# A 64 B store per partition between two large loads of a streaming multiply-and-GELU kernel

## Chip, cores, metric

One core of one Trainium2 chip. The time is device microseconds of one execution; most executions agree within 0.3%. A ratio is the mean time of one kernel's runs over that of the other's of the same rounds, so it is not quite the ratio of the medians quoted beside it.

## The reference

```python
def reference(x, y):                 # both 1024 x 4096 float32
    z = x * y
    return (0.5 * z * (1 + np.tanh(np.sqrt(2 / np.pi) * (z + 0.044715 * z ** 3)))).astype(np.float32)
```

Two arrays of 16.8 MB are read and one is written. There are few operations for each byte.

## The kernel before

Each of 128 partitions holds 8 rows, 32768 floats. The whole of x lies in SBUF, y goes through a buffer of half its size. VectorE multiplies into x, ScalarE applies GELU in place, SyncE issues all transfers on one queue.

```python
X_LOADS = [(0, 16384), (16384, 32768)]
Y_LOADS = [(0, 16384, 0), (16384, 24576, 0), (24576, 32768, 8192)]
STORES = [(0, 16384), (16384, 32768)]
...
    _hoist(nc, [load_x(0).ins, load_y(0).ins])      # ahead of the entry barrier
    load_x(1)
    for i in (1, 2):
        nc.sync.wait_ge(sem_mul, (Y_LOADS[i][1] - Y_LOADS[1][0]) // STEP)
        load_y(i)
...                                                 # 8 multiplies, 8 GELUs of 128x4096
    for i, (a, b) in enumerate(STORES):
        nc.sync.wait_ge(sem_act, b // STEP)
        nc.sync.dma_start(out=out_r[:, a:b], in_=xs[:, a:b]).then_inc(sem_o[i], 16)
```

So the queue runs: x first half, y first half, x second half, third and fourth quarter of y, two stores. I call them x0, y0, x1, y1, y2, s0, s1.

Of the kernel before, what the change touches and what calls it, by code (L numbers as in the profile page):

```python
# [1 line left out]

# [4 lines left out]


F32 = mybir.dt.float32
GELU = mybir.ActivationFunctionType.Gelu_apprx_tanh  # L10


X_LOADS = [(0, 16384), (16384, 32768)]

Y_LOADS = [(0, 16384, 0), (16384, 24576, 0), (24576, 32768, 8192)]
STEP = 4096
STORES = [(0, 16384), (16384, 32768)]
Y_RING = 16384


def _hoist(nc, issued):

    here = nc.cur_bb.bb.instructions
    first = nc.main_func.blocks[0].instructions
    for ins in issued:
        del here[next(k for k, i in enumerate(here) if i is ins or i.name == ins.name)]
    engine = issued[0].engine
    at = next(
        k
        for k, i in enumerate(first)  # L30
        if i.engine == engine and type(i).__name__ == "InstDrain"
    )
    first[at:at] = issued


@with_exitstack
def kernel(
    ctx: ExitStack,
    tc: tile.TileContext,
    x: bass.AP,  # L40
    y: bass.AP,
    out: bass.AP,
):
    nc = tc.nc
    P = nc.NUM_PARTITIONS

    x_r = x.flatten_outer_dims().rearrange("(p a) c -> p (a c)", p=P)
    y_r = y.flatten_outer_dims().rearrange("(p a) c -> p (a c)", p=P)
    out_r = out.flatten_outer_dims().rearrange("(p a) c -> p (a c)", p=P)
    total_f = x_r.shape[1]  # L50


    tc.close()
    tc.compile()  # L54

    xs = nc.alloc_sbuf_tensor("xs", [P, total_f], F32).ap()
    ys = nc.alloc_sbuf_tensor("ys", [P, Y_RING], F32).ap()
    sem_x = [nc.alloc_semaphore(f"sem_x{i}") for i in range(len(X_LOADS))]
    sem_y = [nc.alloc_semaphore(f"sem_y{i}") for i in range(len(Y_LOADS))]
    sem_o = [nc.alloc_semaphore(f"sem_o{i}") for i in range(len(STORES))]  # L60
    sem_mul = nc.alloc_semaphore("sem_mul")
    sem_act = nc.alloc_semaphore("sem_act")

    def load_x(i):
        a, b = X_LOADS[i]
        return nc.sync.dma_start(out=xs[:, a:b], in_=x_r[:, a:b]).then_inc(sem_x[i], 16)  # L66

    def load_y(i):
        a, b, r = Y_LOADS[i]
        return nc.sync.dma_start(  # L70
            out=ys[:, r : r + b - a], in_=y_r[:, a:b]
        ).then_inc(sem_y[i], 16)

    _hoist(nc, [load_x(0).ins, load_y(0).ins])
    load_x(1)
    for i in (1, 2):
        nc.sync.wait_ge(sem_mul, (Y_LOADS[i][1] - Y_LOADS[1][0]) // STEP)
        load_y(i)

    n = 0  # L80
    for i, (a, b, r) in enumerate(Y_LOADS):
        for j, (xa, xb) in enumerate(X_LOADS):
            if xa <= a < xb:
                nc.vector.wait_ge(sem_x[j], 16)
        nc.vector.wait_ge(sem_y[i], 16)  # L85
        for c in range(a, b, STEP):
            nc.vector.tensor_mul(  # L87
                out=xs[:, c : c + STEP],
                in0=xs[:, c : c + STEP],
                in1=ys[:, r + c - a : r + c - a + STEP],  # L90
            ).then_inc(sem_mul, 1)
            n += 1
            nc.scalar.wait_ge(sem_mul, n)
            nc.scalar.activation(  # L94
                out=xs[:, c : c + STEP], in_=xs[:, c : c + STEP], func=GELU
            ).then_inc(sem_act, 1)

    for i, (a, b) in enumerate(STORES):
        nc.sync.wait_ge(sem_act, b // STEP)
        nc.sync.dma_start(out=out_r[:, a:b], in_=xs[:, a:b]).then_inc(sem_o[i], 16)  # L100
    for i in range(len(STORES)):
        nc.sync.wait_ge(sem_o[i], 16)
    nums = sorted(s.num for s in [*sem_x, *sem_y, *sem_o, sem_mul, sem_act])
    assert nums == list(range(nums[0], nums[-1] + 1))
    nc.sync.sem_clear(range(nums[0], nums[-1] + 1))


# [1 line left out]
_INS = ['x', 'y']  # L109
_OUTS = [((1024, 4096), 'float32')]  # L110


# [23 lines left out]
```

## Time and profile before

| | before |
|---|---|
| median at first, 3 runs | 121.02 us (120.82 to 121.17) |
| span of the profiled run | 119.5 us |
| VectorE, ScalarE busy | 29%, 25% |
| share of the span in which packets of the 16 DMA engines ran | 98.5% |

The prediction shows the page and the chain. Two more lines are needed later, from the timeline of the kernel before. The columns are start, duration, engine and line, operation; the bracket at the end is the idle time of the engine before it.

```profile
70.47 8.76 DVE L87 TENSOR_TENSOR xs<-xs,ys 128x4096 f32<-128x4096 f32 x2 [11.70 <-DMA ys<-in_y_dram]
80.88 4.43 DVE L87 TENSOR_TENSOR xs<-xs,ys 128x4096 f32<-128x4096 f32 x1 [1.66 <-DMA ys<-in_y_dram]
```

The bracket of the second line is a gauge. y2 follows y1 on the queue, and 8 rows of 32 KB at 1.21 us take 9.68 us. The two multiplies take 8.76. If the stream ran at its usual rate, VectorE would idle some 0.92 us (the runs below that lose nothing there read 0.95); it idles 1.66. The 0.7 us between is the excess that the prediction found on the last load packets before s0. I call it the late excess.

### The profile page before, as it was taken

How to read it: one execution, taken by the hardware profiler on the slowest of the kernel's cores; microseconds unless marked ns; L12 is line 12 of the kernel's file. 1: busy time of each engine (PE TensorE's matmuls, PEld its weight loads, DVE VectorE, ACT ScalarE, POOL GpSimd, SP SyncE). 2: the span in 40 equal slices, each digit the busy share in tenths (PEclk: the TensorE clock that was granted, in tenths of full speed). 3: DMA queues.
4: the chain of work that ended last, by engine and by line, in shares of the span. 5: the costliest groups of instructions: out<-in, count | busy, mean ns of one | idle time of the engine just before them, and what ended most of it. 6: DMA issues, size and time to landing. Idle time of an engine off the chain costs nothing.

```text
span 119.5 us, 68 instructions
## 1 busy us (share of the span) xinstructions
DVE 35.0 (29%) x8; ACT 30.2 (25%) x9; POOL 0.2 (0%) x4
## 2 busy tenths in 40 slices
DVE  0000000000000199999600049959990000000000
ACT  3000000000000006797780000977479200000000
POOL 0000000000000000000000000000000000000000
DMA  9889888998899889988898989998899888988890
GB/s 351 351 373 680 351 351 351 636 417 351 351 636 417 351 351 526 526 351 351 351 526 351 504 373 482 395 526 351 351 395 658 351 351 351 702 351 351 351 680 22
DMA packets 1008, 50.33 MB, mean 421 GB/s; under 512 B 112, under 2 KB 112, under 8 KB 112
## 3 DMA queue, kind: packets, MB, share of 16 engines
q1 hardware_dynamic: 1008, 50.33, 98.5%
HBM read 33.55 MB, written 16.78 MB: 421 GB/s over the span
## 4 chain that ended last, share of the span: by engine, by line
DMA 53%; DVE 22%; ACT 3%; SPq 0%; issue 0%; DVEq 0%
DMA ys<-in_y_dram 53%; DVE xs L87 22%; ACT xs L94 3%; SPq L66 0%; DVEq L85 0%
## 5 line engine op out<-in xcount | busy, mean ns | idle before, releaser
L87 DVE TENSOR_TENSOR xs<-xs,ys 128x4096 f32<-128x4096 f32 x8 | 35.0, 4421 | 54.7 <-DMA ys<-in_y_dram 54.7
L94 ACT ACTIVATE xs<-xs 128x4096 f32<-128x4096 f32 x8 | 28.9, 3617 | 61.1 <-DVE xs L87 61.1
L94 ACT ACT_TABLE_LOAD x1 | 1.3, 1283 | 1.9 <-PEq L54 1.9
L120 POOL MEMSET const-bfloat16-1.0<- 128x1 bf16 x1 | 0.1, 102 | 0.0
L120 POOL MEMSET const-uint8-127<- 128x1 uint8 x1 | 0.1, 102 | 0.0
L120 POOL MEMSET const-float32-1.0<- 128x1 f32 x1 | 0.1, 99 | 0.0
L120 POOL MEMSET const-float32-0.0<- 128x1 f32 x1 | 0.1, 98 | 0.2 <-issue 0.2
## 6 DMA issues: line engine op xcount, KB each, us to landing
ys<-in_y_dram SPq DMA_DIRECT2D x2, 4096.0 KB, 21.1
xs<-in_x_dram SPq DMA_DIRECT2D x2, 40.3
out_dram<-xs SPq DMA_DIRECT2D x2, 31.9
ys<-in_y_dram SPq DMA_DIRECT2D x1, 40.8
```

Source lines behind the costliest of these rows:

```text
L87: nc.vector.tensor_mul(out=xs[:, c : c + STEP], in0=xs[:, c : c + STEP], in1=ys[:, r + c - a : r + c - a + STEP],).then_inc(sem_mul, 1)
L94: nc.scalar.activation(out=xs[:, c : c + STEP], in_=xs[:, c : c + STEP], func=GELU).then_inc(sem_act, 1)
L120: nc = _bacc.Bacc("TRN2", target_bir_lowering=False, num_devices=1)
```

## The change

It writes 64 B of zeros to the head of each partition's output row, behind y0 and ahead of x1. The first real store overwrites them. An early touch of the output would be of use if the first store had a price of its own that could be paid ahead.

```diff
+    ws = nc.alloc_sbuf_tensor("ws", [P, 16], F32).ap()
+    sem_w = nc.alloc_semaphore("sem_w")
...
+    fill = nc.vector.memset(ws, 0.0).then_inc(sem_mul, 1)
+    _hoist(nc, [fill.ins])
     _hoist(nc, [load_x(0).ins, load_y(0).ins])
+    nc.sync.wait_ge(sem_mul, 1)
+    nc.sync.dma_start(out=out_r[:, :16], in_=ws).then_inc(sem_w, 16)
     load_x(1)
...                       # the counts of sem_mul go up by one
         nc.sync.wait_ge(sem_act, b // STEP)
+        if i == 0:
+            nc.sync.wait_ge(sem_w, 16)
```

More of the change, by code (lines that the diff above doesn't have):

```diff
@@ L72, in load_y @@
         ).then_inc(sem_y[i], 16)
+    fill = nc.vector.memset(ws, 0.0).then_inc(sem_mul, 1)
+    _hoist(nc, [fill.ins])
     _hoist(nc, [load_x(0).ins, load_y(0).ins])
+    nc.sync.wait_ge(sem_mul, 1)
+    nc.sync.dma_start(out=out_r[:, :16], in_=ws).then_inc(sem_w, 16)
     load_x(1)
     for i in (1, 2):
-        nc.sync.wait_ge(sem_mul, (Y_LOADS[i][1] - Y_LOADS[1][0]) // STEP)
+        nc.sync.wait_ge(sem_mul, 1 + (Y_LOADS[i][1] - Y_LOADS[1][0]) // STEP)
         load_y(i)
-    n = 0
+    n = 1
     for i, (a, b, r) in enumerate(Y_LOADS):
@@ L102 @@
         nc.sync.wait_ge(sem_o[i], 16)
-    nums = sorted(s.num for s in [*sem_x, *sem_y, *sem_o, sem_mul, sem_act])
+    nums = sorted(s.num for s in [*sem_x, *sem_y, *sem_o, sem_w, sem_mul, sem_act])
     assert nums == list(range(nums[0], nums[-1] + 1))
```

## The prediction

> **What bounds the kernel now.** I read the page first, then the chain of waits in order of time, the timeline, and last the single packet records of the trace, which no view prints. The page says at once that this is a kernel of transfers.
>
> ```profile
> span 119.5 us, 68 instructions
> DVE 35.0 (29%) x8; ACT 30.2 (25%) x9; POOL 0.2 (0%) x4
> DMA  9889888998899889988898989998899888988890
> DMA packets 1008, 50.33 MB, mean 421 GB/s; under 512 B 112, under 2 KB 112, under 8 KB 112
> q1 hardware_dynamic: 1008, 50.33, 98.5%
> ```
>
> The reader is to see that no compute engine is busy a third of the span, while the 16 DMA engines are busy in every slice to the end and their packets fill 98.5% of the span. Of the 1008 packets 112 are small: 7 transfers x 16 engines, the packets that raise a semaphore. The other 896 are rows of 64 or 32 KB.
>
> ```profile
> 0.00 0.39 SPq L66
> 0.39 0.05 issue
> 0.44 40.80 DMA ys<-in_y_dram
> ...
> 41.34 17.44 DVE xs L87 x4
> 58.78 0.02 issue
> 58.80 21.99 DMA ys<-in_y_dram
> ...
> 80.88 8.77 DVE xs L87 x2
> 89.66 0.02 issue
> 89.68 3.62 ACT xs L94
> ```
>
> This is the chain of waits. It walks through VectorE from 41 to 59 us because it follows semaphores, but that stretch does not set the end: the transfer issued at 58.80 was queued behind others. The timeline shows it:
>
> ```profile
> 50.13 9.00 SPq L70 DMA_DIRECT2D ys<-in_y_dram  x2
> 62.45 31.22 SPq L100 DMA_DIRECT2D out_dram<-xs  x2
> ```
>
> The packet records give the rest. On each engine the order is x first half, y first half, x second half, the third and fourth quarter of y, two stores. A 64 KB packet takes 2.418 us, a 32 KB one 1.213 us, and the next starts as the last ends. The third transfer ends at 59.9 to 60.3 us, but the next was issued at 50.13: slack 9.8 us. The fourth ends at 69.6 to 70.0, the next was issued at 58.80: slack 10.8. The first store was issued at 62.45 and starts near 80.0: slack 17.5. The second was issued at about 93.3 and starts at 99.3: slack 6.0. So the queue never runs dry, and the path that sets the end is simply the sum of packets on the slowest of 16 engines (end at 119.07), plus 0.46 us to the end of the span. As a check: 40 packets x 2.414 spacing + 16 x 1.21 = 115.9; first packet at 1.0 to 1.7; the first packet of each engine takes 0.71 us over the usual (mean); and 0.70 us of excess (mean over engines, 0.59 to 0.81) lies on the last two load packets before the first store, at 76.8 to 80 us. Another 0.15 us is spread over 50 to 58 us. The sum is about 118.8.
>
> **What the Trainium skill says.** (1) "DMA: Bandwidth & Descriptors", section "Specifications", puts 512 B as the least transfer for line rate and says that below this the engine does read-modify-write. The added writes are 64 B, so they fall under it. The trace of before has no such data packet; it can neither agree nor disagree. (2) The same page, "Why small descriptors are slow (HBM only)", gives a fixed overhead of about 3 cycles a packet beside 32 B a cycle; 64 B is then 5 cycles, at the 850 MHz of "Where 436 GB/s comes from" 5.9 ns, an estimate from that page. The trace has only the 4 B semaphore packets to compare: the next packet starts 6 ns after one. (3) The same page, "Queues, rings and completion order", says that each ring is consumed in order and that the semaphore write lands only after every earlier write of that engine. The trace agrees that order costs nothing here: between the two stores, with HBM writes ahead of it, the semaphore packet still takes 6 ns from the stream. (4) "VectorE: DVE Perf Modes", "Zero memsets can be issued as uint32 (trn2)": one cycle per element, so 16 elements are almost only start-up. The four 128x1 memsets on the page take 0.10 us each.
>
> **The change part by part.** Removed: nothing. The same seven large transfers run in the same order with the same bytes.
>
> Added on VectorE: one memset of 128x16 before the entry barrier, some 0.1 us by the 128x1 rows. ScalarE, waiting in the timeline for that barrier, and SyncE both go on at 1.93 us, well after such a memset could end, and VectorE has nothing to do until 41.34. Cost on the path: 0.
>
> Added on SyncE: a wait that is met by then, and one more issue, about 0.33 to 0.43 us by the timeline's rows. The second x load is then issued at about 2.3 instead of 1.93 us, while its turn comes at 40.4. Slack 38 us, cost 0. The first store also waits for the small write's semaphore: that write is over near 41 us, the store is issued at 62.45. Cost 0. All waits on the multiply count are shifted by one, and VectorE's schedule hangs on the y load ahead of the insertion, so it does not move.
>
> Added on the DMA engines: 128 rows over 16 engines, 8 packets of 64 B and one semaphore packet each, between packets that touch each other. The queue has no slack anywhere, so this time is paid in full. Three terms:
> - Throughput: 8 x 6 ns = 0.05 us by the estimate of (2); if a 64 B HBM write takes five times that, 8 x 30 ns = 0.24. I take 0.15.
> - One semaphore packet: 0.006 us.
> - Turning from loads to a store and back. The trace has one such turn, with 0.70 us of excess. I do not know whether it belongs to any turn, or to a large store whose reads run ahead. The only transfers that stand behind the new write are loads, whose reads can start while the small writes are on their way. I take 0.4 of 0.70, that is 0.3 us.
> Sum: 0.15 + 0.01 + 0.3 = 0.46 us, taken as 0.5. Time: 121.02 + 0.5 = 121.5 us, or 0.4% up.
>
> **The rivals.**
> 1. Each 64 B write goes alone: if the engine reads, merges and writes one row before it takes the next, it pays a round trip to HBM eight times. The trace bounds a round trip at the first packet: 0.71 us over its usual time. 8 x 0.71 = 5.7 us, time 126.7, slower. For it: (1) above. Against it: nothing in the trace shows an engine that waits for its own writes; stores stream at the same 2.418 us as loads, and the page tells of packets that are pipelined. A half-way case, one round trip for all eight packets and a full turn each way, would be 0.7 + 0.7 + 0.7 = 2.1 us, time 123.1, still inside 2%.
> 2. The small write takes over the first-store cost: if the 0.70 us at 76.8 to 80 us is a first touch of the output and not a turn, the small write pays it at 40 us and the big store no longer does. The total then grows by 0.15 us alone, or, if the touch is hidden behind the running loads, falls by 0.55 to 120.5. For it: no other start of a transfer (y at 21, x at 40, second store at 99) shows an excess. Against it: the excess lies on load packets ahead of the store, as a change of direction would make it, and the new write touches only the head of each row of 128 KB.
> 3. It is hidden: a few tens of ns go into the spread of the 16 engines (ends from 118.60 to 119.07) and the time stays at 121.0 to 121.2. For it: only the slowest engine counts, and the records show small packets at 6 ns. Against it: all engines get eight packets, so the slowest gets them too.
>
> **Range and chances.** My middle is 121.5. The lower end, 120.8, is rival 2 in part, or rival 3 with the 0.3% of scatter in the three runs. The upper end, 122.9, is the half-way case nearly full. Beyond it stands rival 1, to which I give about one chance in eleven of passing 2% (123.44). A gain of over 2% (118.6) would need 2.4 us off a queue that gets more work: 0.02 for what I don't see. That leaves 0.89.
>
> **What would show it.** In the changed profile: 144 more packets, 1152 in all, 272 of them under 512 B; VectorE x9 with the memset in the first 2 us. The first multiply still starts at 41.3: if it moves, the write or its wait acts ahead of the y load. The landing of the second y load (70.4 before) moves by the cost of the write and that of the third (80.8) by the same; the difference between these two, 10.3 us before, shrinks to 9.7 if rival 2 is right. Packet records of 64 B at 6 to 30 ns from each other would show the throughput term; some 0.7 us apart, rival 1; a longer load packet before or after them, the turn. The prediction is wrong if the time passes 122.9, which a serial write would do, or falls below 120.8.

## The result

The changed kernel took 120.92 us (4 runs, 120.91 to 121.10) against 120.94 (4 runs): ratio 0.9999, interval 0.9981 to 1.0018. I had foreseen 121.5, a ratio of about 1.004. The range and the class (within 2%) held; the forecast of a loss did not.

The page of the changed kernel:

```profile
span 119.7 us, 71 instructions
DVE 35.0 (29%) x9; ACT 30.2 (25%) x9; POOL 0.2 (0%) x4
DMA packets 1152, 50.34 MB, mean 421 GB/s; under 512 B 256, under 2 KB 256, under 8 KB 256
q1 hardware_dynamic: 1152, 50.34, 98.6%
```

There are 144 more packets, as foreseen. The 256 small ones are 128 of 64 B and 128 that raise semaphores; my 272 was a wrong sum (112 + 144 is 256). Its timeline, cut to what the argument needs:

```profile
0.15 0.07 DVE L76 MEMSET ws<- 128x16 f32 x1
...
1.92 0.35 SPq L80 DMA_DIRECT2D out_dram<-ws  x1
...
2.31 0.43 SPq L68 DMA_DIRECT2D xs<-in_x_dram  x1
...
70.39 8.76 DVE L93 TENSOR_TENSOR xs<-xs,ys 128x4096 f32<-128x4096 f32 x2 [11.61 <-DMA ys<-in_y_dram]
```

The memset and the issues lie where they were put, the issues 38 us ahead of need. y1 landed in time for a multiply at 70.39, before at 70.47: no delay. The packet records say what the write itself took. Here are those of one engine of the changed kernel around 40 us, read from the trace:

```
start ns   bytes   to the next start
40860          4        6      (semaphore of y0)
40866         64        7
40873         64        7
...                            (8 of 64 B, each 7 ns on)
40915         64        7
40922          4        6      (semaphore of the small write)
40928      65536     2414      (first row of x1, its usual 2.418 us)
```

So the write takes 8 x 7 + 6 = 62 ns an engine, and the load packets on both sides keep their usual length. No turn shows at 40 us. The late excess is still there: the multiplies on y1 and y2 start 10.59 us apart, before 10.41 (not the 10.3 of my text), where rival 2 wanted 9.7.

```profile
80.98 4.42 DVE L93 TENSOR_TENSOR xs<-xs,ys 128x4096 f32<-128x4096 f32 x1 [1.83 <-DMA ys<-in_y_dram]
```

### The profile page after: what moved, and what is told of

Read it like the earlier page. It is cut to its first block, busy times and chain, and to the rows that moved or that the text cites. A ratio compares the mean times of both kernels' runs of the same rounds, so it can differ in the third digit from the quotient of the medians.

```text
span 119.7 us, 71 instructions
## 1 busy us (share of the span) xinstructions
DVE 35.0 (29%) x9; ACT 30.2 (25%) x9; POOL 0.2 (0%) x4
## 4 chain that ended last, share of the span: by engine, by line
DMA 53%; DVE 22%; ACT 3%; SPq 0%; issue 0%; DVEq 0%
DMA ys<-in_y_dram 53%; DVE xs L93 22%; ACT xs L100 3%; SPq L68 0%; DVEq L91 0%
```

## The experiments

Theories after the result. T: the 62 ns are all that the small write costs, too little to time; there is no turn for it. Rivals: the write gives back about as much as it takes; or it is hidden, whatever its size up to a point; or its price is put off by some buffer. All runs keep the place between y0 and x1 unless told otherwise, and all outputs were correct. Edits are against the changed kernel.

**1. The changed kernel again, five rounds.** No edit.

> The changed kernel itself, in more rounds. My theory now: the small write costs the 0.062 us that the packet records show on each engine (8 packets at 7 ns and one at 6), and there is no turn for so small a store; ratio 1.0005, so 121.0 against 120.95, same. The predicted 0.5 us (with 0.3 us for a turn) would be a ratio of 1.004. Rival: the write warms the output and gives something back; then the 0.70 us of excess at 77 to 80 us shrinks and the ratio is under 0.998.

It took 121.0 us against 120.95, ratio 1.0001 (0.9986 to 1.0015). A loss of 0.4% lies outside. The 0.05% of T cannot be told from nothing.

**2. 64 pieces of 64 B to each row.**

```diff
-    nc.sync.dma_start(out=out_r[:, :16], in_=ws).then_inc(sem_w, 16)
+    nc.sync.dma_start(
+        out=out_r[:, : 2048].rearrange("p (n c) -> p n c", c=32)[:, :, :16],
+        in_=ws.rearrange("p (n c) -> p n c", c=16)).then_inc(sem_w, 16)
```

> The same place, but 64 pieces of 64 B to each row of the output (stride 128 B): 512 small packets an engine. Theory that each costs 7 ns and nothing is hidden: 512 x 7 = 3.58 us, so 124.5 us, ratio 1.030. Rival that the small write is free because it hides in the slack between the engines: that slack is 0.5 us, so some 124.0. Rival that a read-modify-write costs a round trip each, absorbed so far by a buffer of a few packets: many times as much, over 130 us.

It took 127.37, ratio 1.0525 (1.0508 to 1.0541): 6.4 us, or 12.5 ns a packet, more than T. In the packet records the first packets follow each other every 7 ns, but from about 42 us on some 275 instead of 450 start on the 16 engines in 200 ns, so 11.6 ns a packet on each. A price of a round trip each is refuted; the 7 ns do not hold for so many. Nor are the 6.4 us the packets' alone: x1's issue ended only at 45.25 us here (run 13 tells why that matters), and its first packets took 0.80 us longer than usual.

**3. 16 pieces of 512 B.** Edit as in 2, with pieces of 128 floats.

> 16 pieces of 512 B to each row: 128 packets an engine. A packet of 64 KB moves 27.1 B/ns; 512 B at that rate is 19 ns, with the 5 ns that a 64 B packet takes beyond its bytes 24 ns. So 128 x 24 = 3.1 us, 124.0 us, ratio 1.025, and no turn. If pieces below 512 B are dear and those of 512 B are not, the 64 B packets of the other run must be slower than bytes plus overhead, and these 19 ns (2.4 us).

It took 124.51, ratio 1.0285 (1.0268 to 1.0302). The packets start 23 to 24 ns apart, as bytes plus 5 ns said. The rest came as excess: 0.66 us on y0's last packets, while the late excess fell to 0.10. That I had not expected ("no turn").

**4. One piece of 4 KB.** `ws` of 1024 floats, `out_r[:, :1024]`.

> One piece of 4 KB to each row in the same place (as many bytes as the 64 pieces of 64 B): 8 packets of some 151 to 156 ns an engine, 1.2 us. Theory A, the 0.70 us before the first large store belongs to a store whose reads run ahead by some 20 KB: with 32 KB an engine a turn appears, on the last packets of the first y load, total 1.9 us, 122.9. Theory B, it belongs to the end of the loads and not to a change of direction: no excess at 36 to 41 us, total 1.2 us, 122.2, ratio 1.010.

It took 122.20, ratio 1.0103 (1.0087 to 1.0118). Both theories were half right. The last packets before the small store took 0.80 us more, so a turn does appear at 38 us, as A said. But the total is B's 1.2 us, because the late excess has gone:

```profile
82.21 4.43 DVE L93 TENSOR_TENSOR xs<-xs,ys 128x4096 f32<-128x4096 f32 x1 [0.95 <-DMA ys<-in_y_dram]
```

The gauge is at 0.95. The excess was paid once, at the first store that was large enough, although some 39 us of loads (x1, y1, y2) lay between the two.

**5. 16 pieces of 64 B.** Edit as in 2, with 16.

> 16 pieces of 64 B to each row in the place of one: 128 small packets an engine, about as many as went through at 7 ns apart before the 512 of the earlier run fell back to some 11.6 ns. Theory that the 7 ns are paid in full: 128 x 7 = 0.90 us, 121.85 us, ratio 1.0074. Theory that the real price is the 12.5 ns of the long run and that a buffer only puts it off: 1.6 us, 122.55, ratio 1.013. Rival that the small write is free: 1.000.

It took 123.31, ratio 1.0207 (1.0171 to 1.0243): 2.3 us, more than either theory. The small packets again stood 7 ns apart, 0.91 us in all. But then the engines idled 0.50 us on average before x1's first packets, and these took 0.66 us longer than usual. The late excess stayed as well (0.87 us by the packet records; the gauge):

```profile
83.19 4.42 DVE L96 TENSOR_TENSOR xs<-xs,ys 128x4096 f32<-128x4096 f32 x1 [1.94 <-DMA ys<-in_y_dram]
```

Runs 12 to 14 follow this up.

**6. One piece of 1 KB.** `ws` of 256 floats.

> One piece of 1 KB to each row in the same place, 8 KB an engine. With 4 KB pieces the excess of 0.70 us before the first large store moved to 38 us and was gone at 77 to 80. Theory of a read-ahead filled once: stores read ahead by up to 19 KB an engine (0.70 us x 27.1 B/ns) and pay for it once; 8 KB then moves 8192/27.1 = 0.30 us of excess to 38 us and leaves 0.40 us at 77 to 80, sum 0.70; total cost 8 x 45 = 0.36 us, 121.3, ratio 1.003. Rival, a switch that is paid whole or not at all: 0.70 at one place and 0 at the other.

It took 121.09, ratio 1.0013 (0.9994 to 1.0032). The late excess was 0.81 us, not 0.40, with 0.08 early. My read-ahead filled in proportion is refuted.

**7. and 8. HBM to HBM, and SBUF to SBUF, 4 KB a row.**

```diff
+    nc.sync.dma_start(out=out_r[:, :1024], in_=x_r[:, :1024]).then_inc(sem_w, 16)   # 7
+    nc.sync.dma_start(out=wt, in_=ws).then_inc(sem_w, 16)                           # 8, wt: 128x1024
```

> The 4 KB pieces written from the rows of x in HBM instead of from SBUF (the values are wrong until they are overwritten, as the zeros were). If the once-only excess belongs to writing HBM, it moves to 38 us again and the late one is gone. If it belongs to reading SBUF, nothing shows at 38 us and 0.70 us stays at 77 to 80. Total in either case about 1.2 us, ratio 1.010, if a packet takes 155 ns from HBM to HBM as well.

> The 4 KB pieces copied from SBUF to SBUF in the same place; nothing is written to HBM early. If the once-only excess belongs to reading SBUF, it moves to 38 us and the late one is gone; if it belongs to writing HBM, 0.70 us stays at 77 to 80. Total about 1.2 us, ratio 1.010.

They took 122.17 (ratio 1.0101, 1.0083 to 1.0118) and 122.33 (1.0110, 1.0093 to 1.0128). The gauge in the timeline of run 7, then of run 8:

```profile
82.07 4.42 DVE L93 TENSOR_TENSOR xs<-xs,ys 128x4096 f32<-128x4096 f32 x1 [1.80 <-DMA ys<-in_y_dram]
```

```profile
82.33 4.43 DVE L94 TENSOR_TENSOR xs<-xs,ys 128x4096 f32<-128x4096 f32 x1 [0.95 <-DMA ys<-in_y_dram]
```

With HBM as the source nothing showed at 38 us, and the late excess stayed at 0.80. With SBUF as the source and no early write to HBM, 0.91 us came at 36 to 40 us and the late excess was 0. So with pieces of 4 KB the excess goes with the first read from SBUF on the queue, not with writing HBM or a first touch of the output. It is not a matter of bytes alone: the 64 B pieces of run 2 read as many bytes from SBUF, and the late excess was still 0.71.

**9. The 16 small pieces from SBUF to SBUF.** Edit as in 5, into a buffer in SBUF.

> The 128 small packets an engine of the many16 run, but copied from SBUF to SBUF. There the first packets of the second x load took 0.65 us more than usual, beside 0.90 us for the small packets, together 12 ns a piece. If writing pieces of 64 B into HBM has that price, the excess at 40 to 46 us goes and the time falls by about 0.65 us or more, to 122.6; if small packets as such have it, nothing changes against many16 (123.3).

It took 123.32, ratio 1.0189 (1.0166 to 1.0212), the same as run 5. Whatever made run 5 dear is not the writing of 64 B pieces into HBM.

**10. One piece of 2 KB.** `ws` of 512 floats.

> One piece of 2 KB to each row, 16 KB an engine. At 1 KB the late excess stayed whole, at 4 KB it went over whole to 38 us. A switch between 8 and 32 KB an engine would show all of it on one side; a read-ahead that fills bit by bit would show part on each, some 0.4 early and 0.3 late. Packets cost 8 x 83 ns = 0.66 us; total about 121.6, ratio 1.0055.

It took 121.44, ratio 1.0034 (1.0004 to 1.0064). The early excess was 0.40 and the late one 0.03, so in this execution neither a clean switch nor a sum that is kept. The profiled execution was the fastest of four, though (121.08; the others 121.25 to 121.66), so the others may have kept more of the excess.

**11. Two attempts to gain.** The copy from SBUF to SBUF goes to ScalarE's queue ahead of the entry barrier, so that it runs beside the slow first packets.

```diff
+    ready = nc.scalar.wait_ge(sem_mul, 1)
+    copy = nc.scalar.dma_start(out=wt, in_=ws).then_inc(sem_w, 16)
+    _hoist(nc, [ready.ins, copy.ins])
-    nc.sync.wait_ge(sem_mul, 1)                          # and the small store
```

> An attempt to gain by it: the SBUF to SBUF copy of 4 KB a partition goes to ScalarE's queue as soon as the zeros are there (about 1.3 us), so that it runs beside the first load packets, which start slowly anyway (0.71 us over). Theory: the excess at 77 to 80 us (0.70) is gone, because reading from SBUF was begun before; the packets cost 8 x 155 ns = 1.24 us, of which up to 0.7 lies in the slow start. Between 120.8 and 121.6 us, ratio 0.999 to 1.005. Rival: the state does not last through 75 us of loads; the late excess stays, 122.2.

> The same with 2 KB a partition: 8 x 79 ns = 0.63 us, which the slow start could hide whole. If 16 KB an engine are enough to move the excess, and the start hides them, 120.3 us, ratio 0.994; if not enough, 121 to 121.6 with the late excess still there.

They took 122.21 (ratio 1.0105, 1.0080 to 1.0131) and 121.55 (1.0047, 1.0022 to 1.0072). The attempts failed. With 4 KB, load packets started 2.57 us apart instead of 2.42 until the copy was done, with one small packet behind each large one. The first 4 KB packet of any engine started at 6.4 us, so the copy ran behind the slow start and not in it. The late excess stayed (0.72 and 0.96). Whether it stayed because the copy came in single pieces or because it came so early, these two don't tell.

**12. Another look at the kernel before, and 4 and 8 pieces of 64 B.** The pieces are as in 2.

> The kernel before once more, for a second profile. If the late excess differs by chance from run to run, it comes out elsewhere than 0.70 us, between 0.6 and 1.0; if the small write adds 0.2 to 0.3 us to it, it is 0.70 again within 0.05.

> 4 pieces of 64 B to each row, 32 small packets an engine. At the 7 ns of the records 0.22 us, ratio 1.002; at the 18 ns of the run of 128 packets 0.58 us, ratio 1.005. The first packets of the second x load show 0 excess in the first case, some 0.15 us in the second.

> 8 pieces of 64 B to each row, 64 small packets an engine. At 7 ns 0.45 us, ratio 1.004; at 18 ns 1.15 us, ratio 1.0095. If the excess on the second x load begins once a buffer is full, this run shows where between 32, 64 and 128 packets.

The second profile of the kernel before had a late excess of 0.77, and 0.15 spread over 58 to 74 us, against 0.70 and 0.14 (at 50 to 60 us) in the first. That misses the 0.70 within 0.05 of one theory, but does not reach the 0.90 and 1.01 of the changed kernel; two profiles of each don't settle whether the change adds to it. The run with 4 pieces took 121.04 (ratio 0.9996, 0.9982 to 1.0010), the one with 8 took 120.89 (0.9991, 0.9977 to 1.0004). So 64 packets an engine, 0.46 us in the records, cost nothing that shows in the time, and the 18 ns of run 5 do not hold for few packets.

**13. Where the step between 8 and 16 pieces is.** No run, but the issue of the small write and of x1 by SyncE, in the timelines of the runs with 8 and with 16 pieces.

```profile
1.92 0.40 SPq L80 DMA_DIRECT2D out_dram<-ws  x1
2.37 31.15 SPq L68 DMA_DIRECT2D xs<-in_x_dram  x1
```

```profile
1.92 0.40 SPq L80 DMA_DIRECT2D out_dram<-ws  x1
2.37 38.78 SPq L68 DMA_DIRECT2D xs<-in_x_dram  x1
```

Issuing x1 takes 0.43 us beside one piece, 31.15 beside 8, and 38.78 beside 16. With 8 it ends at 33.5, well ahead of need. With 16 it ends at 41.15, when the small packets are already half done. It looks as if x1's descriptors had to wait for room, so that x1 lost its head start and paid a slow start again, as x0 does at the beginning of the kernel (0.71 us).

**14. The same 16 pieces as two transfers of 8, before and after x1.**

```diff
+    small(0, 256)        # 8 pieces of 64 B a row
     load_x(1)
+    small(256, 512)
```

> The 16 pieces of 64 B a row as two transfers of 8, one before the second x load and one after it: as many small packets as the run that cost 2.34 us. If the step is the late issue of the load (no room for its descriptors behind so many), then with 8 pieces ahead the load is issued by some 34 us, there is no idle time before its first packets and no excess on them, and the cost is 128 x 7 = 0.90 us or less: 121.0 to 121.9, ratio under 1.0075. If small packets as such cost 18 ns, it is 123.3 again, ratio 1.02.

It took 121.17, ratio 1.0012 (1.0000 to 1.0025), for as many small packets as in run 5 (1.0207). The timeline of this run:

```profile
2.37 31.18 SPq L68 DMA_DIRECT2D xs<-in_x_dram  x1
33.60 4.85 SPq L81 DMA_DIRECT2D out_dram<-ws  x1
```

x1 is issued by 33.6, and no idle time and no excess stands at its first packets. So small packets as such are not what made run 5 dear. Of the 2.2 us between the two runs, 1.16 are the idle time (0.50) and the excess (0.66) at x1's first packets, which go with the late issue. Run 3 fits this: it too had 128 packets ahead of x1, but they lasted until 44.9 us, x1's issue ended at 42.0, ahead of need, and x1's packets took only 0.14 us more than usual. Another 0.84 us are the late excess, which run 5 kept (0.87) and this run lost (0.03). Why it did is open: the split also moved half of the pieces behind x1. The gauge of this run also reads 0.95:

```profile
81.15 4.42 DVE L100 TENSOR_TENSOR xs<-xs,ys 128x4096 f32<-128x4096 f32 x1 [0.95 <-DMA ys<-in_y_dram]
```

The 128 small packets take 0.98 us in the records, and the time grew by 0.13: most was given back by the late excess. The sums of excess over the usual packet lengths, worked out from the packet records of the profiled runs (us, mean of the 16 engines), side by side. "Early packets" is the time of the added packets themselves; the other columns are excess by its place in the span (35 to 50 us and so on):

```
run                 early packets   excess 35-50   50-74   74-90
before, 1st / 2nd      -                0.01        0.14 / 0.15   0.70 / 0.77
changed, 1st / 2nd     0.06             0.00        0.00          0.90 / 1.01
4 x 64 B               0.23             0.00        0.00          0.75
8 x 64 B               0.46             0.06        0.01          0.58
16 x 64 B, split       0.98             0.07        0.04          0.03
16 x 64 B, in one      0.91             0.66 *      0.03          0.87
16 x 512 B             3.0              0.80        0.01          0.10
1 KB                   0.36             0.08        0.22          0.81
2 KB                   0.65             0.40        0.00          0.03
4 KB from SBUF         1.25             0.80        0.00          0.00
4 KB HBM to HBM        1.25             0.00        0.00          0.80
* and 0.50 idle
```

Small transfers that are read from SBUF can therefore use time that would otherwise be lost before the first large store; with 8 pieces and with the split 16 they used up part or all of it. With 16 pieces in one transfer, into HBM (0.87 late) or into SBUF (0.91), they did not. These rows and that of 1 KB fit no simple rule, and what makes the excess is open.

## Why the prediction was wrong

**What bounds the kernel** held. The queue never ran dry, VectorE's first multiply stayed at 41.35 (41.34 before), and all slacks held. Larger early transfers came out in the time as the sum of packets says: 4 KB a row cost 8 x 156 ns = 1.25 us of packets and 1.25 us of time.

**Memset, issue, waits at no cost**: right, by the timeline above. (The 0.10 us that I took for the memset were rows of POOL; on VectorE it took 0.07.)

**The turn, 0.3 us: this step failed.** I took part of the 0.70 us before the first large store as the price of going from loads to a store and back. Runs 7 and 8 show that it goes with reads from SBUF (pieces of 4 KB there) and not with writing HBM. The 512 B an engine of the change are too few: neither they nor 8 KB in one piece a row made a turn at 40 us of more than 0.08. The term is 0.00.

**Throughput, 0.15 us, was mis-sized.** It measured 8 x 7 ns = 0.056 us. The estimate of 5.9 ns in point (2) of the prediction, which I raised some threefold out of caution, was nearly right.

With these two terms my sum becomes 0.06 us, which five rounds do not resolve. Rival 3's number (121.0 to 121.2) was therefore the best but for 0.1 us. Its reason, hiding in the spread of the engines, is not shown: all engines take the 62 ns, and the ends of the profiled runs moved on average from 118.78 and 118.79 to 118.84 and 118.90.

**Rival 1** (a round trip for each write) is refuted by the 7 ns and by runs 12 and 14. **Rival 2** (first touch of the output) is refuted for this write, which touched the rows and left the late excess at 0.90, and by run 7, which wrote 4 KB of each. Its number, 0.70 us that can be paid earlier, was real, but the reads from SBUF carry it. No version beat either kernel clear of the noise: what an early transfer saved, its own packets cost.

What stays open: the cause of the 0.14 and 0.15 us between 50 and 74 us, which the two profiles of the kernel before and the run of 1 KB (0.22) show, with none in the changed kernel's two; and by what rule the late excess falls. With both counted, the kernel before lost 0.84 and 0.92 us ahead of the first store, the changed one 0.90 and 1.01. Whether the change gives anything back is therefore not known; all together it is within 0.15% of zero.

## What to carry to other kernels

In these runs a tiny transfer in a saturated queue cost its packets, 7 ns for each row of 64 B on its engine, and no round trip; up to 8 such pieces a row it neither helped nor hurt, as it did not delay the issue of what stood behind it beyond need. Watch that issue: with 128 small descriptors an engine ahead of it, the next load was issued too late and 2.3 us were lost, about half of it at that load's first packets. Splitting the same descriptors in two took nearly all of the loss away, though not all by the earlier issue. Before charging a dip seen at one change of direction to every such change, do the half of it alone: reads and writes apart.

## What the Trainium skill lacked or had wrong

- "DMA: Bandwidth & Descriptors", "Specifications", says that transfers below 512 B are done by read-modify-write. No run shows a price for it: 64 B pieces into HBM start 7 ns apart, and 16 pieces a row cost the same into HBM (123.31 us) as into SBUF (123.32 us).
- The same page, "Why small descriptors are slow (HBM only)": an estimate by its 3 cycles at 850 MHz gives 5.9 ns for 64 B and 22.4 ns for 512 B; the runs have 7 and 23 to 24 ns. Its "HBM only" is not borne out for pieces of 64 B: from SBUF to SBUF (run 9) they started 7 ns apart too.
- No page that I read has the room for descriptors on a queue as a number. "Perfetto Trace Analysis", in the section on the HWDGE instruction, only says that a descriptor buffer can fill. The runs don't give one either. An estimate from the issue times: when x1's issue ended at 33.5 us in the run with 8 pieces, 4 descriptors of y0, 65 of the small write and 9 of x1 stood on an engine, 78; in the run with 16, about 70 and 9, 79. But by the same count it was some 107 in run 3, and 141 in run 14 when the issue of the second small transfer ended at 38.45 us (2 of y0, 65, 9 and 65). What the issue waits for is therefore open.
- No page has the 0.7 us that a stream of loads loses once, just before the first large transfer read from SBUF (0.70 to 1.01 us late in the two kernels, or 0.80 and 0.91 us early in runs 4 and 8, and then none late).
